# Activations of the up stage 192 bytes into longer quads, merge and last tiles moved to the weights' place modulo 256

## The chip, the cores and the metric

The kernel runs on one core of a Trainium2 chip. A time is the device time of one execution in microseconds (us); the figure for a kernel is the median of its runs. The profile comes from one further execution, recorded by the hardware profiler. Engines are named as in the profile: PE is TensorE's matmul, PEld its weight load, DVE is VectorE, ACT is ScalarE, POOL is GpSimd, SP is SyncE, whose queue issues most of the DMAs.

## The reference

One decoder block on 512 tokens of 1024 channels, in float32:

```
h = rms_norm(x, g_mix_pre);  z = h @ w_in                      # 1024 -> 4608
y_pool = pool_mixer(z_pool, pool_w, pool_scale) @ w_pool_out
y_rnn  = rg_lru_branch(z_rx, z_rg, ...) @ w_rg_out
merged = sigmoid(z_g0) * y_pool + sigmoid(z_g1) * y_rnn        # the merge
x = x + rms_norm(merged @ w_o, g_mix_post)

h = rms_norm(x, g_ffn_pre)
up = h @ w_up                                                  # 1024 -> 2 * 3072
gate_h = causal_dwconv(up[..., :D_FF], ffn_conv_w, ffn_conv_b)
x = x + rms_norm((gelu(gate_h) * up[..., D_FF:]) @ w_down, g_ffn_post)

ple_gate = sigmoid(rms_norm(x, g_ple_gate) @ w_ple_gate)
x = x + ple_gate * rms_norm(p @ w_ple_proj, g_ple_post)
```

## The kernel before

Every product is made in float32r from operands split in a high and a low part: `split` (L178) casts the high part on ACT and subtracts it on DVE, and `mm3` (L183) issues three matmuls, high by high (L185), and the two mixed ones (L186, L187). In a matmul one operand is loaded into the array (the weights, 128 columns, 512 bytes of each partition, a load of its own on PEld) and the other streams through it (the moving operand, 256 or 512 columns, 1024 or 2048 bytes of each partition). Each matmul loads its own weights, and the load for the next one runs beside the matmul under way.

The order on PE is written out by hand (`manual_schedule`); on the other engines a scheduler orders what the code records, by priority and by the buffers that come free. The stages on PE:

- the in projections (`in_tile`, L544): moving `A` (quads `ht`), weights `hi`/`lo`, 512 columns; between them the heads' gates (L598), with 64 rows and moving `m`, and the pool maps, moving `m`;
- the merge (L808): per channel tile 4 times 3 matmuls with moving `m` (`yp`) and 8 times 3 with moving `C` (`yh`, `yl`), 512 columns;
- the o product (`product`, L749): here `A` is the weights (`of`, L799) and the loaded weights stream, 512 columns; then the PLE projection with `m` as weights (`pq`, L736);
- the up stage (`products`, L889): the activations stream, 256 columns, weights are `hi`/`lo`. The product is a Strassen-like one of seven block products; the forms 1, 2 and 4 of the activations are halves of `h2h`/`h2l` (tiles `C`, L948), the forms 5, 6, 7 and 3 are the tiles `A` of L959. Per pair of channel tiles p there are seven products of 24 matmuls (`up_product`, L965);
- the down product (`down_product`, L1129): like o, with `A` (L1120) as weights, 512 columns;
- the PLE gate (L1226): `x3t` (tiles `h` of the pool `hid`) as weights, moving `hi`/`lo`, 512 columns, and in the very last tile two halves of 256.

Tiles come from pools, laid one after the other in SBUF. `wpool` holds `raw`, `hi`, `lo`, six buffers each. `big` holds four quads `A` and four `C` of 4 x 512 float32 (8192 bytes of a partition; `quad`, L133). `mid` holds 26 slots `m` of 512 float32 (`slot`, L130); a new slot waits until the slot that had its buffer is used up. After the up stage's start `mid` is closed, and `hid` (six quads `h`) takes its room. `small` holds the 16 single columns `s` and the tile `junk`, into which the squares of `rstd_of` (L426) are written, of which only the accumulated sum is used.

A tile's byte address within its partition is fixed when the program is built. In the built program of the kernel before, the tiles `hi`, `lo`, `A` and `C` begin at 192 modulo 256, `m` and `h` at 0. All offsets inside these tiles that a matmul reads from (128, 256 or 512 columns of four bytes) are multiples of 256, so that what a matmul reads has the place of its tile. Below, the **distance** of a matmul is the place of the weights that are loaded beside it (those of the next matmul) less the place of its moving operand, modulo 256:

| stage | moving, weights | columns | matmuls | distance before | distance after |
|---|---|---|---|---|---|
| in, part of the merge | A or C, hi/lo | 512 | 1056 | 0 | 0 |
| o, down | hi/lo, A | 512 | 672 | 0 | 0 |
| pool maps, part of the merge | m, hi/lo | 512 | 108 | 192 | 0 |
| heads' gates | m, C (64 rows) | 512 | 48 | 192 | 0 |
| PLE projection | hi/lo, m | 512 | 48 | 64 | 0 |
| up | A or C, hi/lo | 256 | 2040 | 0 | 64 |
| PLE gate | hi/lo, h | 512 | 168 | 64 | 0 |
| PLE gate, last tile | hi/lo, h | 256 | 48 | 64 | 0 |

(At a change of stage the next weights can be of another tile; such single matmuls are counted with their stage.) Modulo 512 the distances before are 0 where 0 stands and 320 where 64 stands. After, a quad is 256 bytes longer than a multiple of 512, so that the four buffers of `A` and of `C` alternate: in the up stage 1182 matmuls are at 320 modulo 512 and 856 at 64 (two stand at a change of stage), and of the 1728 of 512 columns with `A` or `C` at distance 0, 773 are at 256 modulo 512.

Of the kernel before, what the change touches and what calls it, by code (L numbers as in the profile page):

```python
# [9 lines left out]
F32 = mybir.dt.float32  # L10
F32R = mybir.dt.float32r
# [36 lines left out]
UP_SUMS = (1, 2)  # L48

SUMS_FROM, SUMS_EACH = 3, 6  # L50
URGENT = 700
WARM = 10

# [25 lines left out]
def block_kernel(  # L79
# [24 lines left out]
    wpool = ctx.enter_context(tc.tile_pool(name="wpool", bufs=6))  # L104
    big = ctx.enter_context(tc.tile_pool(name="big", bufs=4))
    tmp = ctx.enter_context(tc.tile_pool(name="tmp", bufs=5))
    small = ctx.enter_context(tc.tile_pool(name="small", bufs=16))
    mid_pool = tc.tile_pool(name="mid", bufs=26)
    mid = mid_pool.__enter__()
    psum = ctx.enter_context(tc.tile_pool(name="psum", bufs=8, space=bass.MemoryType.PSUM))  # L110
    dram = ctx.enter_context(tc.tile_pool(name="dram", bufs=1, space=bass.MemoryType.DRAM))
# [18 lines left out]
    def slot(dt=F32):  # L130
        return mid.tile([P, S], dt, tag="m", name=nm("m"))

    def quad(tag, dt=F32R):  # L133
        return big.tile([P, 4, S], dt, tag=tag, name=nm(tag))

    def tiny(n=1, dt=F32):
        return small.tile([P, n], dt, tag="s", name=nm("s"))
# [178 lines left out]
    def split_early(n):  # L316
        for key in todo[:n]:
            raw = wpool.tile([P, D], F32, tag="raw", name=nm("raw"), bufs=6)
            nc.sync.dma_start(raw.rearrange("p (k c) -> p k c", k=2), src[key])
            hi = wpool.tile([P, D], F32R, tag="hi", name=nm("hi"))  # L320
            lo = wpool.tile([P, D], F32R, tag="lo", name=nm("lo"))
            split(hi, lo, raw)
            for i, v in enumerate((hi, lo)):
                nc.sync.dma_start(parts[key][i], v.bitcast(F32))
        del todo[:n]
# [12 lines left out]
    def up_form(p, f):  # L338

        b = blocks  # L340
        if p == 0:
            t = block(0, f)
        elif p in UP_SUMS:
            t = block(p, {1: 11, 2: 21, 3: 22}.get(f, f))
        elif f == 1:
            for k in (11, 12, 22, 21):
                b[p, k] = block(p, k)
            b[p, 0] = wpool.tile([P, 2, S], F32, tag="sum", name=nm("sum"), bufs=1)
            t = b[p, 11]
        elif f == 6:  # L350
            add(b[p, 0], b[p, 11], b[p, 12])
            t = b[p, 11]
            add(t, b[p, 0], b[p, 22])
        elif f == 7:
            t = b[p, 12]
            add(t, t, b[p, 22])
        elif f == 4:
            t = b[p, 21]
            add(t, b[p, 11], t)
        else:  # L360
            t = b[p, {2: 21, 3: 22, 5: 0}[f]]
        hi = wpool.tile([P, 2, S], F32R, tag="hi", name=nm("hi"))
        lo = wpool.tile([P, 2, S], F32R, tag="lo", name=nm("lo"))
        split(hi, lo, t)
        if p == 1 and f != 1:
            behind(last_copy[0], h2_done[0])
        if p > 2 and f == 6:
            behind(last_copy[0], z_done[0])
        ready["up", p, f] = (hi, lo)

    def prep(key):
        if key[0] == "up" and key not in parts:
            up_form(*key[1:])
            return
        if key in parts:
            hi = wpool.tile([P, D], F32R, tag="hi", name=nm("hi"))
            lo = wpool.tile([P, D], F32R, tag="lo", name=nm("lo"))
            for i, v in enumerate((hi, lo)):
                nc.sync.dma_start(v.bitcast(F32), parts[key][i])
            if key[0] == "up":  # L380
                hi, lo = (v.rearrange("p (j c) -> p j c", j=2) for v in (hi, lo))
            ready[key] = (hi, lo)
            return
        ap = src[key]
        n = 1
        for d in ap.shape[1:]:
            n *= d
        raw = wpool.tile([P, n], F32, tag="raw", name=nm("raw"), bufs=6)
        dst = raw if len(ap.shape) == 2 else raw.rearrange("p (k c) -> p k c", k=ap.shape[1])
        if key == order[0]:  # L390
            nc.sync.dma_start(xraw[0], x_t[0])
            for a, b in FIRST:
                nc.sync.dma_start(raw[:, a:b], ap.rearrange("p k c -> p (k c)")[:, a:b])
        else:
            nc.sync.dma_start(dst, ap)
        hi = wpool.tile([P, n], F32R, tag="hi", name=nm("hi"))
        lo = wpool.tile([P, n], F32R, tag="lo", name=nm("lo"))
        if key == order[0]:
            for a, b in FIRST:
                ACT.copy(hi[:, a:b], raw[:, a:b])  # L400
                sub(lo[:, a:b], raw[:, a:b], hi[:, a:b].bitcast(F32))
        else:
            ACT.copy(hi, raw)  # L403
            with tc.high_priority(offset=2 * URGENT if key[0] == "wpg" and key[2] == 0 else 300 if key[0] == "in" and key[1] >= 12 else 0):
                sub(lo, raw, hi.bitcast(F32))
        ready[key] = (hi, lo)
# [10 lines left out]

    last_pow, last_square = [None], [None]


    def rsqrt(v, n=1):
        y = tiny(n)
# [3 lines left out]
    def rstd_of(halves):  # L426
        sums = []
        for hsrc in halves:
            s = tiny()
            junk = small.tile([P, S], mybir.dt.bfloat16, tag="junk", name=nm("junk"), bufs=1)  # L430
            ins = ACT.activation(junk, hsrc, AF.Square, scale=1.0 / 32.0, accum_out=s)  # L431
            if last_square[0] is not None:
                behind(ins, last_square[0])
            last_square[0] = ins.ins.name
            sums.append(s)
        v = tiny()
        V.scalar_tensor_tensor(v, sums[0], EPS, sums[1], ALU.add, ALU.add)  # L437
        return rsqrt(v)
# [91 lines left out]
    V.tensor_tensor(f, f, s, ALU.add)  # L530
    V.tensor_scalar(ncol, f, -8.0, None, ALU.mult)
    V.tensor_scalar(n2col, f, -16.0, None, ALU.mult)

    rb = const.tile([P, S], F32, tag="rb", name="rb")

    def spread_rstd():
        with urgent():
# [243 lines left out]
    def o_form(f):  # L781

        h11, h12, h21, h22 = (halves(mq[k], b) for b in range(2) for k in range(2))
        v = {1: h11, 2: h12, 4: h22}.get(f)
        if f in (5, 7):
            od[f] = quad("C", F32)[:, 0:2, :].rearrange("p a (b c) -> p (a b) c", b=2)
        if f == 5:
            v = od[5]
            V.tensor_tensor(v, h21, h22, ALU.subtract)
        elif f == 6:  # L790
            v = od[5]
            V.tensor_tensor(v, v, h11, ALU.subtract)
        elif f == 3:
            v = od[5]
            V.tensor_tensor(v, v, h12, ALU.add)
        elif f == 7:
            v = od[7]
            V.tensor_tensor(v, h11, h21, ALU.subtract)
        of[f] = big.tile([P, 2, 4, HALF], F32R, tag="A", name=nm("A"))  # L799
        split(of[f][:, 0], of[f][:, 1], v)  # L800

    def o_lhs(f, k, i):
# [121 lines left out]
    for n, f in enumerate(SERIAL):  # L924
# [20 lines left out]
        if f == 3:  # L945
            x2_norm(0, (o11[0], o12[0]))
            for h in range(2):
                h2h.append(quad("C"))  # L948
                h2l.append(quad("C"))
    x2_sum(2, (oz[0], o5[:, 0]))  # L950


# [3 lines left out]

    forms = {1: h2(0, 0), 2: h2(0, 1), 4: h2(1, 1)}
    for f in (5, 6, 7, 3):
        q = big.tile([P, 2, 4, HALF], F32R, tag="A", name=nm("A"))  # L959
        forms[f] = q[:, 0], q[:, 1]  # L960
    zb = {i: bank() for i in range(2)}
    db = bank()
# [143 lines left out]
    def down_form(f, m):  # L1106
# [10 lines left out]
            V.tensor_tensor(v, v, h12, ALU.add)  # L1117
        elif f == 7:
            V.tensor_tensor(v, h11, h21, ALU.subtract)
        w = big.tile([P, 2, 4, HALF], F32R, tag="A", name=nm("A"))  # L1120
        split(w[:, 0], w[:, 1], v)
        down[f, m] = w

# [199 lines left out]
```

## Time and profile before

| | us |
|---|---|
| median of 3 runs (748.41 to 749.73) | 749.15 |
| the profiled execution | 747.25 |
| its span, first to last instruction | 745.5 |
| PE busy, share of the span | 738.9, 99% |
| PEld busy | 650.7, 87% |
| DVE busy | 577.5, 77% |
| ACT busy | 445.2, 60% |
| POOL busy | 85.3, 11% |
| mean granted clock of TensorE | 1.000 |

A busy PE means that a matmul is under way. Matmuls overlap (one of 256 columns takes 283 ns in the record and the next one starts 120 ns after it), so how fast PE goes is read from the time between starts, not from the busy share or the duration of one.

### The profile page before, as it was taken

How to read it: one execution, taken by the hardware profiler on the slowest of the kernel's cores; microseconds unless marked ns; L12 is line 12 of the kernel's file. 1: busy time of each engine (PE TensorE's matmuls, PEld its weight loads, DVE VectorE, ACT ScalarE, POOL GpSimd, SP SyncE). 2: the span in 40 equal slices, each digit the busy share in tenths (PEclk: the TensorE clock that was granted, in tenths of full speed). 3: DMA queues.
4: the chain of work that ended last, by engine and by line, in shares of the span. 5: the costliest groups of instructions: out<-in, count | busy, mean ns of one | idle time of the engine just before them, and what ended most of it. 6: DMA issues, size and time to landing. Idle time of an engine off the chain costs nothing.

```text
span 745.5 us, 11221 instructions
## 1 busy us (share of the span) xinstructions
PE 738.9 (99%) x4281; PEld 650.7 (87%) x4281; DVE 577.5 (77%) x749; ACT 445.2 (60%) x670; POOL 85.3 (11%) x107
## 2 busy tenths in 40 slices
PE   9999999999999999999999999999999999999997
PEld 7887788888888888889999999999999888887886
DVE  4897545999546568776978998888989998788852
ACT  6747779845433235477866566666666756564721
POOL 0312111100000000110000232313120000011100
PEclk9999999999999999999999999999999999999999
DMA  8998867573978897994533779797979976767011
GB/s 327 383 335 235 229 162 211 114 226 100 323 268 297 302 362 259 309 313 153 180 127 114 280 173 333 196 306 204 290 237 270 322 249 211 261 201 266 17 57 56
DMA packets 64933, 172.53 MB, mean 231 GB/s; under 512 B 5808, under 2 KB 6448, under 8 KB 64560
## 3 DMA queue, kind: packets, MB, share of 16 engines
q1 hardware_dynamic: 50336, 129.78, 49.8%
q0 software_dynamic: 14400, 41.95, 23.7%
q8 instruction: 33, 0.54, 0.3%
q14 instruction: 20, 0.16, 0.1%
q10 hardware_dynamic: 144, 0.10, 0.0%
HBM read 155.03 MB, written 58.72 MB: 287 GB/s over the span
## 4 chain that ended last, share of the span: by engine, by line
PE 96%; DVE 2%; issue 1%; POOL 1%; DMA 1%; ACT 0%; SPq 0%; POOLq 0%; DVEq 0%
PE ps L185 30%; PE ps L187 30%; PE ps L186 30%; PE ps L493 3%; PE ps L850 1%; PE ps L598 1%; DVE lo L176 1%; POOL s L423 1%; DMA raw<-in_w_rx_dram 1%; DVE t L842 0%; DVE C L845 0%; DVE sum L1203 0%; DVE C L1157 0%; ACT hi L403 0%; PE ps L540 0%
## 5 line engine op out<-in xcount | busy, mean ns | idle before, releaser
L176 DVE TENSOR_TENSOR lo<-raw,hi 128x1024 fp32r<-128x1024 f32 (+2 forms) x193 | 224.7, 1184 | 58.1 <-ACT hi L403 34.2
L185 PE MATMUL ps<-A,hi 128*128 128x256 f32 (+1 forms) x608 | 199.9, 329 | 0.0
L187 PE MATMUL ps<-A,lo 128*128 128x256 f32 (+1 forms) x608 | 199.3, 328 | 0.0
L186 PE MATMUL ps<-A,hi 128*128 128x256 f32 (+1 forms) x608 | 199.3, 328 | 0.0
L403 ACT CAST hi<-raw 128x1024 fp32r<-128x1024 f32 (+1 forms) x112 | 112.7, 1015 | 114.9 <-PE ps L186 48.6
L185 PEld LDWEIGHTS ps<-A,hi 128*128 128x128 f32 x608 | 114.5, 188 | 11.1 <-issue 1.1
L187 PEld LDWEIGHTS ps<-A,lo 128*128 128x128 f32 x608 | 114.5, 188 | 10.2
L186 PEld LDWEIGHTS ps<-A,hi 128*128 128x128 f32 x608 | 114.5, 188 | 9.9
L185 PE MATMUL ps<-C,hi 128*128 128x256 f32 (+1 forms) x392 | 118.3, 302 | 0.0
L187 PE MATMUL ps<-C,lo 128*128 128x256 f32 (+1 forms) x392 | 117.9, 301 | 0.0
L186 PE MATMUL ps<-C,hi 128*128 128x256 f32 (+1 forms) x392 | 117.8, 300 | 0.0
L180 ACT CAST hi<-raw 128x1024 fp32r<-128x1024 f32 x78 | 80.8, 1052 | 34.4 <-PE ps L186 32.7
L185 PE MATMUL ps<-hi,A 128*128 128x512 f32 x224 | 87.6, 391 | 0.5 <-DVE sum L1203 0.4
L187 PE MATMUL ps<-hi,A 128*128 128x512 f32 x224 | 87.2, 389 | 0.0
L186 PE MATMUL ps<-lo,A 128*128 128x512 f32 x224 | 87.2, 389 | 0.0
L185 PEld LDWEIGHTS ps<-C,hi 128*128 128x128 f32 x392 | 74.1, 189 | 2.9 <-ACT junk L431 0.3
L186 PEld LDWEIGHTS ps<-C,hi 128*128 128x128 f32 x392 | 74.2, 189 | 2.7
L187 PEld LDWEIGHTS ps<-C,lo 128*128 128x128 f32 x392 | 74.1, 189 | 2.7
L423 POOL TENSOR_TENSOR s<-s,mhalf 128x1 f32<-128x1 f32 (+1 forms) x21 | 18.3, 871 | 336.5 <-DVE s L437 317.8
L259 POOL DMA_DIRECT2D wdsum<-in_w_down_dram x36 | 33.7, 1785 | 149.1 <-ACT t L981 149.1
L185 PEld LDWEIGHTS ps<-hi,A 128*128 128x128 f32 x224 | 42.1, 188 | 9.9 <-DVE sum L1203 0.9
L187 PEld LDWEIGHTS ps<-hi,A 128*128 128x128 f32 x224 | 42.0, 188 | 8.7
(191 smaller groups left out, 1035.3 us busy)
## 6 DMA issues: line engine op xcount, KB each, us to landing
raw<-in_w_up_dram SPq DMA_DIRECT2D x46, 512.0 KB, 6.3
wdsum<-in_w_down_dram POOLq DMA_DIRECT2D x36, 512.0 KB, 12.3
raw<-in_w_in_dram SPq DMA_DIRECT2D x32, 512.0 KB, 7.0
raw<-wdsum SPq DMA_DIRECT2D x24, 512.0 KB, 4.0
raw<-in_w_down_dram SPq DMA_DIRECT2D x18, 512.0 KB, 8.8
wosum<-in_w_o_dram POOLq DMA_DIRECT2D x12, 512.0 KB, 9.3
wdsum<-wdsum POOLq DMA_DIRECT2D x12, 512.0 KB, 10.1
parts<-hi SPq DMA_DIRECT2D x10, 512.0 KB, 4.1
```

Source lines behind the costliest of these rows:

```text
L176: V.tensor_tensor(o, a, b, ALU.subtract)
L180: last_copy[0] = ACT.copy(hi, src)
L185: PE.matmul(o, ah, bh, start=start, stop=False, **kw)
L186: PE.matmul(o, ah, bl, start=False, stop=False, **kw)
L187: PE.matmul(o, al, bh, start=False, stop=stop, **kw)
L259: ins = nc.gpsimd.dma_start(o, i, **kw)
L403: ACT.copy(hi, raw)
L423: last_pow[0] = nc.gpsimd.tensor_tensor(y, v, mhalf[:, :n], ALU.pow).ins.name
L493: PE.matmul(rx[m], a[:, o : o + P], b, start=k == 0 and i == 0, stop=k == KD - 1 and i == 2)
L598: PE.matmul(ps, bd[pr, a, o], b[pr], start=i == 0, stop=i == 2)
L850: PE.transpose(ps[:, q * P : (q + 1) * P], a[:, q * P : (q + 1) * P], ident)
```

## The change

The quads of `big` become 64 float32 (256 bytes) longer, and `quad` takes a place at which the 4 x 512 floats begin. The quads `h2h`, `h2l` and the forms of the up stage are laid at 48 floats (192 bytes), all others at 0. To make room and to set where the pools begin, `mid` has 25 slots for 26, `small` has 22 columns for 16, and the tile `junk` is gone: the squares go into `rb`, a tile of float32 that is used in the in stage and free afterwards. The tiles `hi` and `lo` are now always allocated with 1024 floats and cut. With this `m` and `h` begin at 192 modulo 256, `hi` and `lo` as before at 192, the quads of the up stage at 128, the other quads at 192.

```diff
+PLACES, PLACE_UP = 64, 48
...
-    small = ctx.enter_context(tc.tile_pool(name="small", bufs=16))
-    mid_pool = tc.tile_pool(name="mid", bufs=26)
+    small = ctx.enter_context(tc.tile_pool(name="small", bufs=22))
+    mid_pool = tc.tile_pool(name="mid", bufs=25)
...
-    def quad(tag, dt=F32R):
-        return big.tile([P, 4, S], dt, tag=tag, name=nm(tag))
+    def quad(tag, dt=F32R, place=0):
+        t = big.tile([P, 4 * S + PLACES], dt, tag=tag, name=nm(tag))
+        return t[:, place : place + 4 * S].rearrange("p (a c) -> p a c", a=4)
+
+    def parts_of(n):
+
+        return [wpool.tile([P, D], F32R, tag=t, name=nm(t))[:, :n] for t in ("hi", "lo")]
...
-        hi = wpool.tile([P, n], F32R, tag="hi", name=nm("hi"))
-        lo = wpool.tile([P, n], F32R, tag="lo", name=nm("lo"))
+        hi, lo = parts_of(n)
...
+    rb = const.tile([P, S], F32, tag="rb", name="rb")
...
-            junk = small.tile([P, S], mybir.dt.bfloat16, tag="junk", name=nm("junk"), bufs=1)
-            ins = ACT.activation(junk, hsrc, AF.Square, scale=1.0 / 32.0, accum_out=s)
+            ins = ACT.activation(rb, hsrc, AF.Square, scale=1.0 / 32.0, accum_out=s)
...
-    rb = const.tile([P, S], F32, tag="rb", name="rb")
...
-        of[f] = big.tile([P, 2, 4, HALF], F32R, tag="A", name=nm("A"))
+        of[f] = quad("A").rearrange("p (s a) (b c) -> p s (a b) c", s=2, b=2)
...
-                h2h.append(quad("C"))
-                h2l.append(quad("C"))
+                h2h.append(quad("C", place=PLACE_UP))
+                h2l.append(quad("C", place=PLACE_UP))
...
-        q = big.tile([P, 2, 4, HALF], F32R, tag="A", name=nm("A"))
+        q = quad("A", place=PLACE_UP).rearrange("p (s a) (b c) -> p s (a b) c", s=2, b=2)
...
-        w = big.tile([P, 2, 4, HALF], F32R, tag="A", name=nm("A"))
+        w = quad("A").rearrange("p (s a) (b c) -> p s (a b) c", s=2, b=2)
```

On PE and POOL the same instructions stand in the same order. With a slot of `mid` less, the scheduler orders a few instructions on SP, DVE and ACT otherwise, all between the in stage and the o product. Two places follow.

On SP, at the end of the merge, where the loads of `x` into slots of `mid` (L861, L864 after) stand among the loads of the o product's weights (`wosum`). Before:

```order
L861 DMA m_2437<-in_x_dram 128x512
L395 DMA raw_2456<-wosum_104 128x1024
L861 DMA m_2439<-in_x_dram 128x512
L861 DMA m_2441<-in_x_dram 128x512
L395 DMA raw_2474<-wosum_104 128x1024
L395 DMA raw_2494<-wosum_105 128x1024
L395 DMA raw_2517<-wosum_105 128x1024
L861 DMA m_2443<-in_x_dram 128x512
L861 DMA m_2445<-in_x_dram 128x512
L395 DMA raw_2684<-in_w_ple_proj_dram 128x2x512
```

After:

```order
L400 DMA raw_2456<-wosum_104 128x1024
L864 DMA m_2437<-in_x_dram 128x512
L864 DMA m_2439<-in_x_dram 128x512
L400 DMA raw_2474<-wosum_104 128x1024
L400 DMA raw_2494<-wosum_105 128x1024
L864 DMA m_2441<-in_x_dram 128x512
L864 DMA m_2443<-in_x_dram 128x512
L864 DMA m_2445<-in_x_dram 128x512
L400 DMA raw_2517<-wosum_105 128x1024
L400 DMA raw_2680<-in_w_ple_proj_dram 128x2x512
```

The last of the four `wosum` loads moved behind the last three loads of `x`; the loads of `x` moved later by one or two places.

On DVE, in the in stage, where gate tiles are scaled out of PSUM into slots of `mid` (`m<-ps,rb`, L554, after L557) among the decay of the recurrent branch (L620 to L627, after L623 to L630). Before:

```order
L554 TENSOR_TENSOR m_1138<-ps_1113,rb 128x512
L554 TENSOR_TENSOR m_1192<-ps_1167,rb 128x512
L620 SCALAR_TENSOR_TENSOR m_996<-t_1049,m_996 128x512
L676 MEMSET t_1294 128x16
L176 TENSOR_TENSOR lo_1310<-raw_1307,hi_1309 128x1024
L620 SCALAR_TENSOR_TENSOR m_1002<-t_1055,m_1002 128x512
L625 MEMSET m_685 128x1
L626 TENSOR_TENSOR m_685<-m_685,m_450 128x512
L625 MEMSET m_691 128x1
```

After:

```order
L557 TENSOR_TENSOR m_1138<-ps_1113,rb 128x512
L623 SCALAR_TENSOR_TENSOR m_996<-t_1049,m_996 128x512
L679 MEMSET t_1294 128x16
L184 TENSOR_TENSOR lo_1310<-raw_1307,hi_1309 128x1024
L623 SCALAR_TENSOR_TENSOR m_1002<-t_1055,m_1002 128x512
L628 MEMSET m_685 128x1
L629 TENSOR_TENSOR m_685<-m_685,m_450 128x512
L628 MEMSET m_691 128x1
L557 TENSOR_TENSOR m_1192<-ps_1167,rb 128x512
```

One gate tile (`m_1192`) is taken out of PSUM seven instructions later, when the first slot of the decay's inputs is used up.

## Rows read from the trace of the kernel before

**Rows 1.** The page: busy time, granted clock in 40 slices, chain that ended last

```profile
PE 738.9 (99%) x4281; PEld 650.7 (87%) x4281; DVE 577.5 (77%) x749; ACT 445.2 (60%) x670; POOL 85.3 (11%) x107
PEclk9999999999999999999999999999999999999999
PE 96%; DVE 2%; issue 1%; POOL 1%; DMA 1%; ACT 0%; SPq 0%; POOLq 0%; DVEq 0%
```

**Rows 2.** Groups by shape on PE: line, names, shapes xcount | busy us, mean ns | idle

```profile
L185 PE MATMUL ps<-A,hi 128*128 128x256 f32 x352 | 99.7, 283 | 0.0
...
L185 PE MATMUL ps<-C,hi 128*128 128x256 f32 x328 | 93.1, 284 | 0.0
...
L185 PE MATMUL ps<-hi,h 128*128 128x512 f32 x56 | 22.2, 397 | 0.0
```

**Rows 3.** PE in three stretches (up, down, PLE gate): us, busy (instructions), clock, DMA

```profile
372.80:577.33 204.53, 204.53 (x1706) 1.00 0.81 230
583.00:670.00 87.00, 87.00 (x385) 1.00 0.74 246
...
718.00:735.00 17.00, 17.00 (x75) 1.00 0.12 46
```

**Rows 4.** PE in order of time, last tile: start us, duration, line, shapes

```profile
735.70 0.28 PE L185 MATMUL ps<-hi,h 128*128 128x256 f32 x1
...
740.69 0.28 PE L187 MATMUL ps<-hi,h 128*128 128x256 f32 x1
```

**Rows 5.** PE in order of time, merge's moving m, and the PLE projection

```profile
213.09 0.40 PE L185 MATMUL ps<-m,hi 128*128 128x512 f32 x1
...
215.85 0.40 PE L185 MATMUL ps<-C,hi 128*128 128x512 f32 x1
...
318.11 0.40 PE L185 MATMUL ps<-hi,m 128*128 128x512 f32 x1
...
323.71 0.49 PE L850 MATMUL ps<-ident,m 128*128 128x128 f32 x3
```

**Rows 6.** All engines in stretches of one pair p and before: PE, PEld, DVE, ACT, POOL

```profile
355.20:372.80 17.60, 17.60 (x147) 17.54 (x146) 16.04 (x21) 14.81 (x25) 0.00 (x0) 1.00 0.51 174
...
416.00:436.16 20.16, 20.16 (x170) 20.16 (x169) 17.70 (x20) 12.64 (x20) 4.16 (x7) 1.00 0.72 258
...
557.12:577.28 20.16, 20.16 (x170) 20.16 (x169) 20.04 (x22) 14.48 (x21) 3.44 (x4) 1.00 1.09 267
```

**Rows 7.** Groups on ACT in the up stage, 415 to 577 us: who ended the idle

```profile
L180 ACT CAST hi<-raw 128x1024 fp32r<-128x1024 f32 x44 | 45.5, 1052 | 23.9 <-PE ps L186 22.2 <-DVE raw L336 1.2 <-DMA raw<-in_w_up_dram 0.4
```

**Rows 8.** DVE and PE in order of time, where the down product begins

```profile
549.78 1.22 DVE L336 TENSOR_TENSOR raw<-raw,raw 128x1024 f32<-128x1024 f32 x1
...
585.72 1.22 DVE L176 TENSOR_TENSOR A<-h,A 128x1024 fp32r<-128x1024 f32 x1
...
588.23 0.39 PE L185 MATMUL ps<-hi,A 128*128 128x512 f32 x1
```

**Rows 9.** DVE, SP, ACT and PE in order of time, from the in stage to o

```profile
123.09 1.28 DVE L554 TENSOR_TENSOR m<-ps,rb 128x512 f32<-128x512 f32 x2
...
129.47 0.06 DVE L625 MEMSET m<- 128x1 f32 x1
...
267.31 1.63 SPq L395 DMA_DIRECT2D raw<-wosum  x3
271.52 0.81 SPq L861 DMA_DIRECT2D m<-in_x_dram  x2
...
290.81 0.58 ACT L431 ACTIVATE junk<-ps 128x512 bf16<-128x512 f32 x1
...
294.49 0.58 ACT L939 COPY sum<-ps 128x512 f32<-128x512 f32 x1
...
296.79 0.39 PE L185 MATMUL ps<-hi,A 128*128 128x512 f32 x1
```

More of the change, by code (lines that the diff above doesn't have):

```diff
@@ L319, in split_early @@
             nc.sync.dma_start(raw.rearrange("p (k c) -> p k c", k=2), src[key])
-            hi = wpool.tile([P, D], F32R, tag="hi", name=nm("hi"))
-            lo = wpool.tile([P, D], F32R, tag="lo", name=nm("lo"))
+            hi, lo = parts_of(D)
             split(hi, lo, raw)
@@ L361, in up_form @@
             t = b[p, {2: 21, 3: 22, 5: 0}[f]]
-        hi = wpool.tile([P, 2, S], F32R, tag="hi", name=nm("hi"))
-        lo = wpool.tile([P, 2, S], F32R, tag="lo", name=nm("lo"))
+        hi, lo = (v.rearrange("p (j c) -> p j c", j=2) for v in parts_of(D))
         split(hi, lo, t)
@@ L375, in prep @@
         if key in parts:
-            hi = wpool.tile([P, D], F32R, tag="hi", name=nm("hi"))
-            lo = wpool.tile([P, D], F32R, tag="lo", name=nm("lo"))
+            hi, lo = parts_of(D)
             for i, v in enumerate((hi, lo)):
```

## Prediction

> **What bounds the kernel now.** I read the page first: PE is busy 99% of the span, 96% of the chain that ended last is PE, and the granted clock is full in every slice [rows 1]. A busy PE could still hide waiting, so next the groups by shape: the matmuls of the up stage and of the wide stages have no idle time ahead of them [rows 2]. What is left is the pace, that is the time from start to start, and this I took from long stretches. A stretch counts the one or two matmuls that began before it, which I take off.
>
> - Up stage, 256 columns, distance 0: 204.53 us for 1704 matmuls, 120.0 ns each [rows 3].
> - Down, 512 columns, distance 0: 87.00 us for 383.5, 226.9 ns [rows 3].
> - PLE gate, 512 columns, distance 64: 17.00 us for 73, 233 ns [rows 3]. The PLE projection, the other stage at 64, takes 5.60 us for 24, 233 ns [rows 5].
> - Merge with moving `m`, distance 192: 2.76 us for 12, 230 ns [rows 5].
> - Last tile, 256 columns, distance 64: from the fourth of its 48 matmuls to the last, 4.99 us for 44, 113.4 ns [rows 4].
>
> At the same width and the full clock the pace goes with the distance, and with the width the sign turns: 64 is 6 ns worse than 0 at 512 columns and 6.6 ns better at 256. The busy stages are not the slow ones: the wide matmuls of the quiet PLE gate (DMA share 0.12) are slower than those of the down product (0.74). So I take the place, and not the company of other engines, as what sets it.
>
> **The up stage.** The 2040 matmuls, six groups of 352 or 328 [rows 2], go from distance 0 to 64. If they take the last tile's pace, 2040 x (120.0 - 113.4) = 13.5 us go. The bounds: no stretch of 256 columns shows another value, so the nearest rows are the last tile on the one side (-13.5) and, with the opposite sign, the wide rows, where 64 costs 6 to 6.6 ns (+13.5). I take the last tile, as it has both the width and the distance.
>
> A rule speaks against all of it. The Trainium skill, TensorE: Matmul & The Clock Gate, section "Step-by-step: what each phase is for", says that PE has two independent read ports, and that loading the next tile's weights takes no read bandwidth from the running matmul. By it a place could not matter and this term would be nought; the 120.0 and 113.4 ns of the same width here do not agree with it.
>
> **The wide and last tiles.** 168 matmuls of the PLE gate and 48 of the PLE projection go from 64 to 0: 216 x 6.4 = 1.4 us less (233.3 against 226.9). 108 with moving `m` go from 192 to 0: 108 x 3.1 = 0.3 us less. The last tile's 48 go the other way, from 64 to 0: 48 x 6.6 = 0.3 us more. The heads' 48 half-height matmuls go from 192 to 0, which no row shows; at 6.6 ns each they bound it to 0.3 us either way, and I take 0. Sum with the up stage: -13.5 - 1.4 - 0.3 + 0.3 = -14.9 us.
>
> **Does the rest keep up.** A pair p takes 20.16 us now and would take 19.05. DVE works 17.70 us in a usual pair [rows 6], 93% of the new time, so it still fits. The casts of the weights wait for PE to give buffers back, 22.2 of their 23.9 us of idle time, and hardly for DMA (0.4) [rows 7]: with a faster PE these waits shrink first. Two places have little cover.
>
> - The start of the up stage (355 to 373 us), where DVE works 16.04 and ACT 14.81 of 17.60 us [rows 6], in chains with PE. Some 336 matmuls lie from 330 to 373 us, worth 2.2 us of the gain. Between 0 and 2.2 lost, I take 0.5, since PE hardly waits there now.
> - The end of it. DVE works 20.04 of the last 20.16 us [rows 6], and the third split form of the hidden activations is ready at 586.94 us, 1.3 us ahead of its first matmul at 588.23 [rows 8]. PE would come 5.5% sooner over the some 27.5 us for which DVE has worked without a break (549.78 to 577.3), that is 1.5 us, while DVE has the same work. So 0.2 us is lost at least by this, all 1.5 at most; I take 0.3.
>
> That makes -14.1 us.
>
> **The slot less and the other moves.** PE's order is unchanged. On DVE one gate tile is taken out of PSUM behind the row that now starts at 129.47 us in place of 123.7 [rows 9]: its PSUM bank stays taken 6 us longer. An in tile fills one bank in 24 x 227 ns = 5.4 us, and there are eight banks, so I cost it at nothing; were the other seven taken, PE would wait up to 6 us. On SP the last `wosum` load moves from about 268.6 us, the end of its group's issues, to behind the loads of `x` that wait until 271.52 [rows 9]. It goes out some 4 us later, and its first matmul is at 296.79 [rows 9], over 20 us away: nothing, and the loads queued behind it are for later products still. The loads of `x` are for the norms after the o product. The squares written in float32 in place of bf16: 0.58 us for the one and 0.58 for a copy into float32 of the same shape [rows 9]: nothing. The columns of `small` are off any path that ends last.
>
> **The time.** The profiled execution took 747.25 us, 745.5 of them span; it would take 733.2. The median of the runs lies 1.9 us above the profiled one, and 749.15 - 14.1 = **735.0 us** is the forecast.
>
> **Rivals.**
>
> 1. *The place does not matter* (the skill's rule above, or something else that differs in the last tile, as that its engines are quiet). Then up stays at 120.0 and so do the others: 749 us, no change. Against it: the sign at 512 columns, where the quiet stage is the slower one. Chance 0.08.
>
> 2. *Slower: the distance acts by what stands in the stream.* The last tile differs from the up stage in which operand is the activation, and it is a short stretch of 5 us. If what counts at distance 64 is the sign of the long wide stretches, the up stage pays 6.6 ns more: 2040 x 6.6 = +13.5, less the 1.4 of the wide tiles, 761 us. It decides when a matmul of the up stage takes over 120.7 ns, where the cost outweighs the 1.4. For it: 256 and 512 columns already differ in sign, so the mechanism is not one that I can work out, and 64 costs in two stages of three. Against it: at 512 columns distance 0 gives 226.9 ns with `A` streaming and with `A` as weights alike, so the role does not matter there. Chance 0.11.
>
> 3. *The pattern repeats after 512 bytes and not 256.* Before, all distances were 0 or 320 modulo 512, apart from the 192. After, 1182 of the up stage's are at 320, which the last tile shows, but 856 at 64, and 773 wide ones at 256, which nothing shows. The first gain 1182 x 6.6 = 7.8 us; if the second gain nothing and the 773 lose 3 ns (half of what 64 costs), 2.3 us, the sum is -7.8 - 1.4 + 2.3 = -6.9: 742 us. Chance 0.09.
>
> 4. *The gain is given back to DVE*, 93% busy, by waits all along the up stage: PE would go at the pace of DVE's 17.70 us only if this were over 19.05, which it isn't; a wait for the last forms is in the forecast. No chance of its own.
>
> **How the numbers follow.** The forecast, 0.72. The range: its lower end is the full 14.9 without losses, 734.3, less 0.7 for the scatter of the runs (748.41 to 749.73) and some 1.5 for the changes of stage, where the pace now is off for a few matmuls: 732.0. Its upper end takes in rival 3 with its uncertain price: 745.0. What is left out are rivals 1 and 2, 0.19 together. A measurement of this kernel tells about 0.2% from no change. Faster by more than that: 0.72 + 0.09 and a little of rival 1, 0.82; within it 0.07; slower 0.11.
>
> **What would show it.** In the profile after, a stretch of the up stage gives its pace: 113.4 ns (19.05 us a pair) for the forecast, 120.0 for rival 1, over 120.7 for rival 2, two paces by buffer of `A` and `C` for rival 3, whose mark would also be wide products at two paces. The PLE gate should show 227 in place of 233 ns, the last tile 120 in place of 113.4. DVE's idle time in the up stage should shrink to a twentieth, and a PE wait of up to 1.5 us may stand ahead of the third form of the down product. The forecast is wrong if the last tile's pace is not that of a long stretch with other engines at work.

## The result, and the profile after

The changed kernel took 742.41 us (median of 4 runs, 742.21 to 743.13) against 749.30 us (748.41 to 749.73) for the kernel before beside it: a ratio of 0.9911, 95% interval 0.9894 to 0.9929. It is faster, by 6.9 us where 14.1 were forecast; the time lies inside the range of 732 to 745. Its profiled run took 742.25 us, 740.4 of them span, against 745.5 before. Medians are over runs at the full granted clock: one of the four runs of the first kernel under Experiments took 806.07 us at a mean granted clock of 0.851 and is left out of its median.

First the page (busy time, granted clock, chain). It answers [rows 1] and reads the same: PE is the bound, at full clock, with 92% of the chain in place of 96%.

```profile
PE 733.0 (99%) x4281; PEld 646.1 (87%) x4281; DVE 577.0 (78%) x749; ACT 444.6 (60%) x670; POOL 85.4 (12%) x107
...
PEclk9999999999999999999999999999999999999999
...
PE 92%; DMA 3%; DVE 3%; POOL 0%; ACT 0%; issue 0%; SPq 0%; DVEq 0%; POOLq 0%
```

The stretches, as in [rows 3]: us, PE busy (matmuls), PEld, DVE, ACT, POOL, granted clock, DMA share, GB/s. The first three lie in the up stage, then down, then the PLE gate.

```profile
330.21:335.87 5.66, 5.66 (x50) 5.65 (x48) 4.30 (x9) 3.90 (x10) 1.09 (x2) 1.00 0.94 321
...
343.46:369.08 25.62, 25.62 (x228) 25.62 (x227) 25.12 (x34) 22.30 (x37) 0.00 (x0) 1.00 0.39 135
371.02:571.70 200.68, 200.68 (x1705) 200.68 (x1704) 178.72 (x192) 129.27 (x204) 39.58 (x48) 1.00 0.82 236
583.00:670.00 87.00, 86.98 (x385) 71.68 (x384) 75.84 (x76) 57.24 (x71) 4.16 (x3) 1.00 0.68 234
712.00:729.00 17.00, 17.00 (x77) 14.08 (x76) 5.49 (x8) 2.29 (x4) 0.00 (x0) 1.00 0.13 49
```

With the matmuls that began before a stretch taken off, the up stage runs at 117.8 ns from 371.02 us on (200.68 us for 1704), where it had 120.0; but for 25 us ahead of that it runs at 113.4 (25.62 for 226), the value forecast for all of it. Down stays at 227, and the gate goes from 233 to 227 ns. The moving `m` of the merge (214.19 to 215.55), the PLE projection (321.84 to 323.65) and the last tile (730.48 to 735.64), as in [rows 4, 5], in order of time on PE:

```profile
214.19 0.39 PE L193 MATMUL ps<-m,hi 128*128 128x512 f32 x1
...
215.55 0.39 PE L193 MATMUL ps<-m,hi 128*128 128x512 f32 x1
...
321.84 0.39 PE L193 MATMUL ps<-hi,m 128*128 128x512 f32 x1
...
323.65 0.39 PE L195 MATMUL ps<-hi,m 128*128 128x512 f32 x1
...
730.48 0.28 PE L194 MATMUL ps<-lo,h 128*128 128x256 f32 x1
...
735.64 0.28 PE L195 MATMUL ps<-hi,h 128*128 128x256 f32 x1
```

That is 1.36 us for 6 and 1.81 for 8, 227 ns, and 5.16 for 43, 120.0 ns: all as forecast. So the pace that falls short is that of the up stage, and its long part begins at one instruction. PE in order of time at 370 us; L974 was L971 before:

```profile
370.56 0.28 PE L194 MATMUL ps<-C,hi 128*128 128x256 f32 x1
370.67 0.28 PE L195 MATMUL ps<-C,lo 128*128 128x256 f32 x1
370.79 0.39 PE L974 MATMUL ps<-hi 128*128 128x512 f32 x1
371.02 0.28 PE L193 MATMUL ps<-C,hi 128*128 128x256 f32 x1
371.13 0.28 PE L194 MATMUL ps<-C,hi 128*128 128x256 f32 x1
371.25 0.28 PE L195 MATMUL ps<-C,lo 128*128 128x256 f32 x1
```

L974 is the single 512-column matmul that opens a PSUM bank at `p == 2`, with the weights tile as both operands. Ahead of it the starts lie 0.113 us apart, behind it 0.118 (1704 matmuls), and no wait stands there.

Where the time went, from the first matmul of each stage to that of the next in the two traces (the line between the last two rows is the first transposes for the gate, at 684.47 and 678.98 us, ahead of the last 36 matmuls of down):

| stage | before, us | after, us | difference |
|---|---|---|---|
| to the o product | 279.11 | 279.47 | +0.36 |
| o, PLE projection | 51.08 | 50.74 | -0.34 |
| up | 247.14 | 241.50 | -5.64 |
| down without its last 36 | 107.14 | 107.27 | +0.13 |
| last 36 of down, gate, last tile, end | 61.00 | 61.46 | +0.46 |
| span | 745.47 | 740.44 | -5.03 |

The profiled run of before lay 1.9 us below the median of its own runs, hence -5.0 here and -6.9 by the medians. In the first row the first tiles, which wait for DMA, end 1.4 us later (29.9 against 28.5; 28.7 to 30.1 in the profiles of the experiments), and the rest of in and merge is 1.0 faster: 0.3 from the first pool map to the merge (46.53 to 46.24 us) and 0.7 in the merge (66.03 to 65.28), while the heads' four groups take 1.59 us each in place of 1.60. In the last row the gate's gain is gone: PE waits where it had not waited before. PE, then DVE, in order of time at 694 to 702 us:

```profile
700.47 0.39 PE L195 MATMUL ps<-hi,h 128*128 128x512 f32 x1
701.60 1.32 PE L853 MATMUL ps<-ident,h 128*128 128x128 f32 x8 [0.75 <-DVE h L1160]
...
694.54 0.68 DVE L845 TENSOR_TENSOR t<-ps,C 128x512 f32<-128x512 f32 x1
...
700.87 1.28 DVE L1160 TENSOR_TENSOR h<-C,C 128x512 f32<-128x512 f32 x2
```

From its first row to its last the norm on DVE takes 7.61 us, as before (699.11 to 706.72 there). But it begins 15.6 us after the first transposes in place of 14.6: PE has come closer to DVE, and waits for the transposes' source (1.14 us from start to start at 700.47).

### The profile page after: what moved, and what is told of

Read it like the earlier page. It is cut to its first block, busy times and chain, and to the rows that moved or that the text cites. A ratio compares the mean times of both kernels' runs of the same rounds, so it can differ in the third digit from the quotient of the medians.

```text
span 740.4 us, 11213 instructions
## 1 busy us (share of the span) xinstructions
PE 733.0 (99%) x4281; PEld 646.1 (87%) x4281; DVE 577.0 (78%) x749; ACT 444.6 (60%) x670; POOL 85.4 (12%) x107
## 4 chain that ended last, share of the span: by engine, by line
PE 92%; DMA 3%; DVE 3%; POOL 0%; ACT 0%; issue 0%; SPq 0%; DVEq 0%; POOLq 0%
PE ps L193 30%; PE ps L194 30%; PE ps L195 30%; DMA C<-in_x_dram 1%; DMA A<-pled 1%; DVE lo L184 1%; PE ps L601 1%; DMA m<-in_x_t_dram 1%; PE ps L498 1%; PE ps L853 1%; DVE A L1234 1%; POOL s L429 0%; DVE h L184 0%; DVE t L845 0%; ACT C L481 0%
## 5 line engine op out<-in xcount | busy, mean ns | idle before, releaser
L193 PE MATMUL ps<-C,hi 128*128 128x256 f32 (+1 forms) x392 | 117.0, 299 | 0.0
L194 PE MATMUL ps<-C,hi 128*128 128x256 f32 (+1 forms) x392 | 116.7, 298 | 0.0
```

Source lines behind the costliest of these rows:

```text
L193: PE.matmul(o, ah, bh, start=start, stop=False, **kw)
L194: PE.matmul(o, ah, bl, start=False, stop=False, **kw)
```

## Experiments

Paces are from the starts of the matmuls in each trace. "The wide matmul" is L974.

**The wide matmul taken out of the up stage.** Two 256-column matmuls that stream the activations at distance 64 take its place.

```diff
-PE.matmul(gb[i], w[0][:, 0, :P], w[0][:, 0, :], start=True, stop=True)
+for a in (0, HALF):
+    PE.matmul(gb[i][:, a : a + HALF], w[0][:, 0, :P], forms[1][0][:, 0, :],
+              start=a == 0, stop=True, skip_group_check=True)
```

> Theory, two rhythms: at distance 64 the matmuls of 256 columns have two steady paces, 113.4 and 117.8 ns; a wait of PE leads into the first, a wide matmul at distance 0 into the second, and PE stays in the one it is in. In the changed kernel the one wide matmul at the start of pair 2 (L974) stands ahead of all of the 1704 matmuls at 117.8 ns. Here it is replaced by two of 256 columns at distance 64. Then these 1704 go at 113.4 ns: 7.4 us less than the changed kernel, 735.0 us. Rival, company: the pace of 117.8 ns comes from the DMA and DVE traffic of the pairs from 371 us on. Then it stays at 117.8 ns, and the time at 742.4 us. Rival, DVE: PE is held by DVE; then waits of PE appear and the time lies between.

Measured: 738.77 us, the median of three, against 748.70 for before, ratio 0.9875 (0.9855 to 0.9895). In its stretches (columns as above) the pace is 113.4 ns to 549 us, 179.53 us for 1584:

```profile
343.41:369.04 25.63, 25.63 (x229) 25.63 (x227) 25.14 (x34) 22.31 (x37) 0.00 (x0) 1.00 0.39 131
369.48:549.01 179.53, 179.53 (x1586) 179.53 (x1585) 161.91 (x175) 116.42 (x185) 37.08 (x48) 1.00 0.82 239
```

The up stage takes 235.3 us, 11.8 less than before and 6.2 less than after. Not all of it arrives: down takes 109.4 in place of 107.3 us. What PE waited for from 540 to 590 us (engine, line and releaser: us in total, times, longest), where the kernel after shows nothing:

```profile
PE ps L195 <- DVE A L184: 0.7, 1, 0.7
PE ps L193 <- ACT ps L982: 0.6, 1, 0.6
PE ps L193 <- ACT ps L1185: 0.4, 1, 0.4
PE ps L193 <- ACT A L188: 0.3, 1, 0.3
```

From start to start these places cost some 2.6 us more than the pace.

**The wide matmul put back later**, at `p == 7`, into that kernel.

```diff
+if p == 7 and i == 0:
+    PE.matmul(gb[i], w[0][:, 0, :P], w[0][:, 0, :], start=True, stop=True)
```

> As the kernel with the narrow claim, and one wide matmul at distance 0 (the line that was replaced) at the start of pair 7, whose result is overwritten. Two rhythms: 113.4 ns for the pairs up to 6, 117.8 ns from pair 7 to the end of the up stage, with nothing else changed between them; 735.0 + 864 x 4.4 ns = 738.8 us. Company: the same pace before and after pair 7, whatever it is.

Measured: 738.46 us. Three stretches, the last from the wide matmul on:

```profile
343.00:369.20 26.20, 26.20 (x225) 26.20 (x224) 25.03 (x34) 22.09 (x36) 0.00 (x0) 1.00 0.41 140
369.58:466.27 96.69, 96.69 (x855) 96.69 (x854) 87.92 (x96) 63.37 (x102) 15.39 (x20) 1.00 0.70 218
466.50:568.26 101.76, 101.76 (x866) 101.76 (x864) 91.82 (x99) 65.27 (x103) 23.91 (x30) 1.00 0.97 261
```

96.69 us for 853 is 113.4 ns, 101.76 for 864 is 117.8. The slow rhythm (117.8 ns, against the fast one of 113.4) begins where the wide matmul is. The first stretch shows something else: this kernel has the same instructions up to 369 us as the one above, and runs at 117.8 ns there, until two longer steps from start to start, 0.16 and 0.22 us, at 369.20. So the wide matmul is not all.

**The up stage alone** (nothing else shifted), and the same **without the wide matmul**.

```diff
-small = ctx.enter_context(tc.tile_pool(name="small", bufs=22))
+small = ctx.enter_context(tc.tile_pool(name="small", bufs=16))
...
+junk = small.tile([P, S], mybir.dt.bfloat16, tag="junk", name=nm("junk"), bufs=1)
-ins = ACT.activation(rb, hsrc, AF.Square, scale=1.0 / 32.0, accum_out=s)
+ins = ACT.activation(junk, hsrc, AF.Square, scale=1.0 / 32.0, accum_out=s)
```

> The up stage's quads moved as in the changed kernel, with the squares in junk and 16 columns of small, so that m and h begin at 0 modulo 256 as before. Expected by the distances: the up stage as in the changed kernel (117.8 ns after pair 2 begins), the PLE gate back at 233 ns, the last tile back at 113.4, the merge's moving m at 230. The wide tiles are then worth 1.4 + 0.3 - 0.3 us by their paces. If the wait of 1.1 us that the changed kernel shows at 700 us ahead of the transposes of the last token tile is only the PLE gate's gain given back, it is gone here, and the PLE gate with the transposes takes as long as in the changed kernel to within 0.5 us; if it has another cause it stays and this kernel is 1.1 us longer there.

> The kernel with the up stage alone shifted, in which the up stage ran at 117.8 ns also in front of the single 512-column matmul; here this matmul is replaced by two of 256 columns over activations at distance 64. Theory A (the wide matmul is the only thing that puts the stage into the slower rhythm, and a stretch keeps what it has): the up stage stays at 117.8 ns, since it has that before the replaced matmul, and the time stays at 743 to 744 us. Theory B (the two narrow matmuls themselves start the faster rhythm): 113.4 ns from the place of the replaced matmul, and 739 to 741 us. Theory C (only a wide matmul in the stretch costs, whatever was ahead): 113.4 ns in the whole stretch, and about 738 us.

Measured: 743.48 and 741.36 us. The first (two stretches, ahead of the wide matmul and behind it) has 117.8 ns in both, 26.62 us for 226 and 200.68 for 1704:

```profile
344.30:370.92 26.62, 26.62 (x228) 26.62 (x227) 25.18 (x34) 22.51 (x37) 0.00 (x0) 1.00 0.41 135
372.83:573.51 200.68, 200.68 (x1705) 200.68 (x1704) 178.47 (x192) 128.85 (x203) 39.53 (x48) 1.00 0.82 234
```

The second has 113.8, 117.9, 113.4 and 113.3 ns in these stretches, which breaks of PE (longer steps from start to start) part:

```profile
331.09:336.55 5.46, 5.46 (x50) 5.46 (x48) 3.66 (x9) 3.61 (x9) 1.08 (x2) 1.00 0.92 304
338.11:343.66 5.55, 5.55 (x49) 5.55 (x49) 1.82 (x6) 3.88 (x12) 1.08 (x2) 1.00 0.50 190
344.65:370.27 25.62, 25.62 (x228) 25.62 (x227) 25.12 (x34) 22.31 (x37) 0.00 (x0) 1.00 0.39 131
370.72:512.17 141.45, 141.45 (x1250) 141.45 (x1249) 126.72 (x138) 91.45 (x145) 28.32 (x36) 1.00 0.77 229
```

None of the three theories foresaw a change at a break, so the comparison that this pair was made for does not count; the breaks do. The gate runs at 233 ns in both kernels, and yet from the end of down to the end the first takes the 61.0 us of before: the gate's gain in the kernel after is lost again.

**The wide tiles alone**: `PLACE_UP` at 0, the rest as changed.

```diff
-PLACES, PLACE_UP = 64, 48
+PLACES, PLACE_UP = 64, 0
```

> The changed kernel with the activations of the up stage at place 0 again, so that only the wide tiles (merge, gate, projection) and the last tile are shifted: up stage at 120.0 ns, gate and projection at 227 ns. By the prediction's terms for the wide tiles 1.4 us less than the kernel before; by the trace after, in which the gate's 1.1 us came back as a wait for the norm near the end, 0.2 to 0.8 us less: 748.0 to 748.8 us against some 749.0.

Measured: 746.71 us against 749.26, ratio 0.9969 (0.9958 to 0.9981): 2.3 us less, 1.4 to 3.1 by the interval, and more than expected. Up takes 247.0 us at 120.0 ns; the end takes 60.4 in place of 61.0 us, with no wait named at the transposes. Without a faster up stage the gate's gain does arrive. The wait seems to go with how far PE is ahead of DVE, and not with the gate alone: the kernel with two narrow matmuls, which waits at the start of down, has none here (end 60.2 us), and "up alone, two narrow" steps 0.78 us here with the gate at 233 ns. The up shift then brought the rest of the 6.9 us, 4.6 (alone it gave 5.2 by its one run, 743.48 against 748.70).

**Width or distance of the odd matmul?** In three kernels L974 streams the activations at distance 64 but with 512 columns; it is split in two of 256 at its own distance 0; it is split in four of 128 at distance 64.

```diff
-PE.matmul(gb[i], w[0][:, 0, :P], w[0][:, 0, :], start=True, stop=True)
+PE.matmul(gb[i], w[0][:, 0, :P], h2h[0][:, 0, :], start=True, stop=True)
...
+for a in (0, HALF):
+    PE.matmul(gb[i][:, a : a + HALF], w[0][:, 0, :P], w[0][:, 0, :HALF], start=a == 0, ...)
...
+for a in range(0, S, P):
+    PE.matmul(gb[i][:, a : a + P], w[0][:, 0, :P], h2h[0][:, 0, a : a + P], start=a == 0, ...)
```

> The changed kernel; the single 512-column matmul inside the up stage streams a wide tile at distance 64 instead of distance 0. If its width is what puts the stage into the slower rhythm: 117.8 ns behind it, and 742 to 743 us. If its distance is: 113.4 ns goes on behind it, and 737 to 740 us, as with the two narrow matmuls at distance 64.

> The changed kernel; the single 512-column matmul inside the up stage is split into two of 256 columns, which stream the same weights tile at distance 0 as it did. If the width is what puts the stage into the slower rhythm: 113.4 ns goes on, 737 to 740 us. If the distance is (a single matmul at distance 0, of whatever width): 117.8 ns behind it, 742 to 743 us.

> The changed kernel; the single 512-column matmul inside the up stage is split into four of 128 columns. If only a wide matmul changes the rhythm: that in front goes on behind. If any matmul of another width does: 113.4 ns in front turns to 117.8 ns behind (or the reverse).

Measured: 743.82, 743.04 and 740.52 us. The wide one at distance 64 (stretch ahead, stretch behind): 113.4 ns turns to 117.8.

```profile
342.75:368.38 25.63, 25.63 (x228) 25.63 (x227) 25.13 (x34) 22.31 (x37) 0.00 (x0) 1.00 0.39 129
370.31:571.00 200.69, 200.69 (x1706) 200.69 (x1704) 177.15 (x191) 127.54 (x202) 39.54 (x48) 1.00 0.82 235
```

Its time is above that of the kernel after at the same pace, since PE also waits at the start of down (steps of 1.11 and 0.79 us at 582 and 588 us). With the four of 128, 113.4 ns goes on behind them, at 113.3:

```profile
371.19:547.78 176.59, 176.59 (x1560) 176.59 (x1559) 158.09 (x170) 113.32 (x182) 34.86 (x45) 1.00 0.81 238
```

The pair at distance 0 could not tell, since 117.8 ns stood in the whole stage, ahead of it too. So it ran again, together with the pair at distance 64 on the same chip:

> The same kernel as the one with two 256-column matmuls at distance 0 in place of the wide one, once more; its first look showed 117.8 ns from 330 us on, ahead of the replaced matmul too, so that it could not tell. If the rhythm is drawn at breaks and a narrow matmul doesn't touch it: the same spread and median as its twin at distance 64, 737 to 743 us. If one matmul at distance 0 puts the stage into 117.8 ns: every run at 742 to 744 us.

> The same kernel as the one with two 256-column matmuls at distance 64 in place of the wide one, once more. If the rhythm of the up stage is drawn anew at each break of PE and then kept: single times spread over 736 to 744 us, a profiled run with 113.4 ns throughout lies near 737 and one with 117.8 ns near 743. If the rhythm follows from the code: every run is at 737 to 740 us and shows 113.4 ns.

Measured: the pair at distance 0 took 742.32 us (741.28 to 742.53), ratio 0.9912 (0.9897 to 0.9927); the pair at distance 64 took 739.43 us (738.65 to 740.71), ratio 0.9875 (0.9856 to 0.9893). The ranges do not overlap, against the theory that a narrow matmul touches nothing. This time the first one's trace shows the turn. PE in order of time, L975 being the pair:

```profile
370.48 0.28 PE L193 MATMUL ps<-C,hi 128*128 128x256 f32 x1
370.59 0.28 PE L194 MATMUL ps<-C,hi 128*128 128x256 f32 x1
370.70 0.28 PE L195 MATMUL ps<-C,lo 128*128 128x256 f32 x1
370.82 0.39 PE L975 MATMUL ps<-hi 128*128 128x256 f32 x2
371.05 0.28 PE L193 MATMUL ps<-C,hi 128*128 128x256 f32 x1
371.17 0.28 PE L194 MATMUL ps<-C,hi 128*128 128x256 f32 x1
```

113.4 ns up to it, 117.8 behind it to the end of the stage. So either will do: a width of 512 columns, or another distance (though this pair also streams the very tile that is its weights, which is not told apart from the distance).

The other one, at 113.3 ns from 370 to 548 us, still took 740.20 us in its profiled run, because PE then waits longest there. PE in order of time behind the end of the up stage, and the stretch 581.01 to 583.57:

```profile
577.43 0.39 PE L195 MATMUL ps<-hi,A 128*128 128x512 f32 x1
578.96 0.50 PE L193 MATMUL ps<-hi,A 128*128 128x512 f32 x1 [1.15 <-ACT A L188]
579.30 0.40 PE L194 MATMUL ps<-lo,A 128*128 128x512 f32 x1
580.41 0.80 PE L195 MATMUL ps<-hi,A 128*128 128x512 f32 x1 [0.72 <-DVE A L184]
...
581.01:583.57 2.56, 2.56 (x7) 1.98 (x6) 2.56 (x3) 2.56 (x4) 0.00 (x0) 0.50 0.86 306
```

With the waits at 548 and 550 us (0.79 and 1.08 from start to start) and down at 111.2 in place of 107.3 us, some 5.6 us are given back.

**A shorter matmul behind the wide one.**

```diff
 PE.matmul(gb[i], w[0][:, 0, :P], w[0][:, 0, :], start=True, stop=True)
+PE.matmul(gb[i][:, :P], w[0][:, 0, :P], h2h[0][:, 0, :P], start=False, stop=True, ...)
```

> The changed kernel with its single 512-column matmul, and one of 128 columns straight behind it. If the slower rhythm is a lag that a wide matmul leaves between weight loads and streams, and a shorter matmul gives it back: 113.4 ns behind the pair, 737 to 740 us. If a wide matmul fixes the rhythm until PE next breaks off: 117.8 ns, 742 to 743 us.

Measured: 742.28 us, 113.4 ns ahead and 117.8 behind. It gives nothing back.

**Other places.** The up stage at distance 128 with the in, merge, o and down stages at 128 or 192; then, on the changed kernel, the up stage at 192 with the wide matmul and without it, and at 32 without it.

```diff
-PLACES, PLACE_UP = 64, 48
+PLACES, PLACE_UP = 64, 32
-hth = [quad("A"), quad("A")]
-htl = [quad("A"), quad("A")]
+hth = [quad("A", place=32), quad("A", place=32)]
+htl = [quad("A", place=32), quad("A", place=32)]
...
-yh[i], yl[i] = quad("C"), quad("C")
+yh[i], yl[i] = quad("C", place=16), quad("C", place=16)
...
-of[f] = quad("A").rearrange("p (s a) (b c) -> p s (a b) c", s=2, b=2)
+of[f] = quad("A", place=32).rearrange("p (s a) (b c) -> p s (a b) c", s=2, b=2)
...
-w = quad("A").rearrange("p (s a) (b c) -> p s (a b) c", s=2, b=2)
+w = quad("A", place=48).rearrange("p (s a) (b c) -> p s (a b) c", s=2, b=2)
```

Distances 192 and 32 (without the wide matmul, it is replaced as in the first experiment):

```diff
-PLACES, PLACE_UP = 64, 48
+PLACES, PLACE_UP = 64, 16
...
-PLACES, PLACE_UP = 64, 48
+PLACES, PLACE_UP = 64, 56
```

> Other distances, one for each stage: in stage 128 (512 columns, A streams), merge's moving C 192, o product 128, down product 192 (512 columns, A is the weights), up stage 128 (256 columns). If only the distance modulo 256 and the width count, in and o have one pace, and merge and down have one pace, of some 230 ns as the 108 matmuls at 192 had before. For 256 columns at 128 there is no row: between 113 and 127 ns. If the role of the operand counts, the in and o products differ.

> The changed kernel with the activations of the up stage 64 bytes into their quads, so at distance 192, the wide 512-column matmul in its place. If distance 192 has one rhythm only, as distance 0 does: one pace in front of the wide matmul and behind it, below 117.8 ns if it is a better place (737 to 741 us), above it if not (742 to 749 us). If it has two rhythms, as distance 64 does: two paces in the up stage, the slower one behind the wide matmul.

> The same at distance 192, with two 256-column matmuls over the activations in place of the wide one. One rhythm: the same pace as with the wide one. Two rhythms: the faster of the two for long stretches, redrawn at breaks of PE only.

> The activations of the up stage 224 bytes into their quads (distance 32), two 256-column matmuls over them in place of the wide one. If the pace goes by steps of 64 bytes: as at distance 0, 120.0 ns and 746 to 748 us, or as at distance 64, 113.4 or 117.8 ns and 737 to 743 us. If it goes by 32 bytes or finer: another pace.

Measured: 750.43, 742.42, 745.15 and 744.05 us. (The 745.15 has the pace of the 742.42, but steps of 0.64, 1.11 and 0.79 us at the start of down.) A stretch of the up stage at distance 128, at 192 (with the wide matmul), and at 32:

```profile
378.60:580.79 202.19, 202.19 (x1706) 202.19 (x1704) 179.28 (x193) 129.89 (x204) 39.52 (x48) 1.00 0.82 233
...
370.98:571.66 200.68, 200.68 (x1705) 200.68 (x1704) 178.45 (x192) 128.94 (x203) 39.58 (x48) 1.00 0.82 234
...
369.92:573.09 203.17, 203.17 (x1719) 203.17 (x1719) 180.04 (x194) 129.99 (x204) 39.59 (x48) 1.00 0.82 234
```

That is 118.7 ns at 128 (120.0 in two short stretches ahead), 117.8 at 192 in every stretch with the wide matmul or without, and 118.3 at 32 (203.17 us for 1717). At 512 columns distance 128 gives 232 ns in the in stage, where the activations stream, and 233 in o, where they are the weights; distance 192 gives 229 ns both in the merge and in down, where the roles differ likewise. So of the five places 192 is the sure one for 117.8 ns, 64 alone showed 113.4, and a step of 32 bytes tells.

The paces at distance 64 side by side, in ns. PE breaks off between the first four columns (at the transposes of 336 and 343 us, at the longer steps of 369); the last is behind L974 or what stands for it:

| kernel | 331 | 337 | 343 | 369 | behind |
|---|---|---|---|---|---|
| after | 118 | 113 | 113 | 113 | 118 |
| two narrow at 64 | 118 | 113 | 113 | 113 | 113, 118 after a wait at 549 |
| the same again | 118 | 118 | 118 | 113 | 113 |
| wide at `p == 7` | 118 | 118 | 118 | 113 | 113, 118 behind the wide one |
| up alone | 113 | 113 | 118 | 118 | 118 |
| up alone, two narrow | 113 | 118 | 113 | 113 | 113 |
| wide at 64 | 118 | 113 | 113 | 113 | 118 |
| two narrow at 0 | 118 | 118 | 118 | 118 | 118 |
| the same again | 118 | 113 | 113 | 113 | 118 |
| four of 128 | 118 | 113 | 113 | 113 | 113 |
| wide, then 128 | 118 | 113 | 113 | 113 | 118 |

The pace changed at 11 of these 33 breaks, in either direction, with the same instructions on both sides. The same kernel run twice went different ways. Away from a break it changed only at an odd matmul (one of another width or distance than its neighbours), and only to 118. The first column goes with what came ahead without a break: a wide stage at distance 64 (the two kernels "up alone") gave 113, one at distance 0 gave 118, nine of nine. That is not the rule of a single matmul: one wide matmul at distance 64 inside the stage turned 113 to 118.

## Why the prediction was right in its sign and not in its size

- **PE bounds, and the place sets its pace**: right. Rival 1 falls: with nothing but places moved, 120.0 became 117.8 and 113.4 ns, and 233 became 227. The Trainium skill, TensorE: Matmul & The Clock Gate, section "Step-by-step: what each phase is for", with its two independent read ports, is not borne out here; by what way the place acts, no run shows.
- **The up stage, 2040 x (120.0 - 113.4) = 13.5 us**: the step that failed. The sign and the mechanism stand, but the last tile's pace [rows 4] was taken for that of the distance, and it is one of two rhythms. The stage gave 5.6 us: 1704 of the 2040 matmuls ran at 117.8, 1704 x 4.4 = 7.5 us short. [rows 4] is a stretch entered from wide tiles at distance 64, which gave the fast rhythm in the "up alone" kernels too. The prediction doubted whether a short stretch speaks for a long one, but looked for the danger in its other engines and not in how it is entered or in the one odd matmul in the middle of the up stage. Taking that matmul out restored 113.4 ns, which shows the cause.
- **Wide tiles -1.4, moving `m` -0.3, last tile +0.3**: each pace is as forecast (227, 227, 120.0). But the moving `m` brought 1.0 us in place of 0.3, as in the merge the 24 matmuls with `C` behind each 12 with `m` also quickened, from 228.9 to 226.7 ns, at distance 0 in both kernels: the first ten or so behind `m` had started 0.224 to 0.236 us apart. The heads gave nothing, as forecast. That makes some -2.1 in all, and alone these shifts bring 2.3 us (1.4 to 3.1). In the kernel after the gate's part did not arrive: the end takes 61.5 us against 61.0.
- **Does the rest keep up, 0.8 us**: under-sized, and rival 4, given no chance, is there in part. In the kernel after nothing is lost at the two places named. DVE is busy for all of the last pair, 20.17 of 20.18 us:

```profile
551.52:571.70 20.18, 20.18 (x173) 20.18 (x173) 20.17 (x22) 14.05 (x22) 4.32 (x5) 1.00 1.08 264
```

  The third form of the hidden activations, 1.3 us early in [rows 8], is now 0.5 us early (DVE ends it at 582.16; its first matmul starts at 582.63). But DVE's work has not shrunk, and the gate's 1.1 us come back as the wait at 700 us. Where PE kept 113.4 ns to 548 us, 2.6 us and 5.6 us came back at 548 to 584 us in the two traces of the kernel with two narrow matmuls, over the bound of 1.5 given for this place. Kernels at 117.8 ns lose up to 2.2 us at the start of down in some traces (down takes 109.4 us with two narrow at 192), so the cover is thin there even without the faster pace. So even at the forecast pace the gain is nearer to 10 than to 14.1 us: the two medians of that kernel give 9.9 and 9.6. The sign that DVE's idle time would shrink to a twentieth does not follow from 17.70 of 19.05 us, which leaves 7%; after, DVE works 178.72 of 200.68 us.
- **The slot less, SP's and DVE's moves, the squares in float32, at nothing**: no new wait of PE stands at them. The first tiles' 1.4 us is the scatter of a stretch that waits for DMA.
- **Rival 2**, slower, falls: the role of the operand hardly matters (233 ns with the activations as weights and 232 with them streaming, at 512 columns and distance 128; 229 for both at 192). **Rival 3** gave nearly the measured time, 742, for a wrong reason: no stage splits into paces by buffer, and distances 0 and 256 modulo 512 both give 227 ns. That the time lies inside the range is owed to the upper end, which was set for this rival.

Not settled is what chooses the rhythm when PE starts again after a break: kernels with the same instructions up to there, and one kernel run twice, went either way. That the pair at distance 0 and the wide one at distance 64 turn the rhythm rests on one trace each, and on the times of the former.

## What to carry to other kernels

A pace read from one short stretch is a pace of that stretch: look how it was entered, and what odd instruction stands in the long stretch to which it is to be carried. A place in SBUF was worth 5% of a matmul stream here (120.0 against 113.4 ns); shift one operand, read the pace from the trace, and keep odd widths and places out of the stream. The best version here does both: the change with two narrow matmuls in place of the wide one, 739.4 us against 749.0. And when the bound engine gets faster, price again every place where an engine beside it had no idle time left.

## What was not expected of the hardware

- At 256 columns and distance 64 there are two steady rhythms at the same granted clock of 1.00, 113.4 and 117.8 ns, held for up to 1585 and 1704 matmuls. At distance 0 only 120.0 was seen (the same wide matmul changes nothing there), at 192 only 117.8, at 32 only 118.3.
- The waits that PE's speed brought cost more than their length in two traces. In the second run of the kernel with two narrow matmuls, behind waits of 1.15 and 0.72 us, the granted clock of 581.01 to 583.57 us was 0.50, the lower level of 1.2 GHz, and 512 columns took 427 ns in place of 227, some 1.7 us in eight matmuls. The kernel with four of 128 shows the same (the line below), behind steps of 1.29 and 1.12 us; "up alone, two narrow", with steps of 1.29 and 1.12 us there as well, kept 1.00.

```profile
579.88:582.87 2.99, 2.99 (x9) 2.32 (x8) 2.99 (x3) 2.99 (x4) 0.00 (x0) 0.50 0.94 343
```
